# A hybrid attention layer: merge factors stored and loaded on another queue, exponents made in PSUM, two statistics steps moved

## The chip, the cores and the metric

The kernel runs on one core of one Trainium2 chip. The metric is device time in microseconds (us). The core has five engines with a queue of instructions each: PE (matmul), DVE (vector), ACT (scalar), POOL (GpSimd) and SP, which here only starts transfers (DMA). An engine works its instructions in order. A transfer is started by an instruction on the queue of SP or ACT and then runs by itself.

## The reference

One decoder layer for a prompt of 2048 positions and 32 sample rows, all in float32. For the part that matters here, each of 8 heads takes three dilated windows over the prompt, (128, 1), (512, 4) and (2048, 16), and the branch outputs are merged by their softmax denominators:

```
s = jnp.einsum('bnqrhc,bnkrhc->bnrhqk', qb, kc) * (HEAD_DIM ** -0.5) + bias
s = jnp.where(valid, s, NEG_INF)
lse = logsumexp(s, axis=-1)
o = einsum(exp(s - lse), vc)
...
w = jax.nn.softmax(jnp.stack(lses, axis=0), axis=0)
att = jnp.sum(w[..., None] * jnp.stack(outs, axis=0), axis=0)
...
x = x + jnp.concatenate([att, u * gate], axis=-1) @ w_out
x = x + _swiglu(x, norm2_g, w_gate, w_up, w_down)
```

Before it stands a projection of x to q, k, v, u and the gate; behind it the output projection and the feed-forward part.

## The kernel before

The stages follow each other: projections (to some 600 us of the span), attention over the prompt's heads (600 to 965), a junction in which the first block's output projection begins (to 1075), then output projection and feed-forward in three blocks of positions to the end. Each stage is written out by hand: `at(step, phase, fn)` puts a function into a plan, and the plan emits the instructions sorted by step and by phase, in the order early, exp, low, scores, turn, mid, values, out, misc, store. There is no reordering later; each engine's order is the order of emission.

In attention one step is one item. An item is a block of 128 queries of one head over its dense and 4-strided keys together ("band", at most 640 keys), or four residues of the 16-strided window ("strided"); there are 16 of the one and 4 of the other, 20 steps per head. For an item at step x, PE makes the scores (L864 band, L941 strided), DVE adds the bias and takes the maximum at x+1 (L870, L946 and L948), POOL subtracts it for strided items (L949), ACT takes the exponential (L875 at x+2, L952 at x+3), PE transposes the result (L891 at x+3, L961 at x+4), ACT and DVE copy it out of PSUM (L896, L963, L902), and PE multiplies with the values (L918, L970). DVE sums the strided item's exponentials (`strided_sum`, L956) at x+4. POOL gathers the strided keys and queries of an item, three casts (L933), two steps ahead of its scores.

When a head is done, `Stats` combines the statistics of its two parts in the next head's steps (s0 is that head's first step). `a` spreads the band part's maxima and sums over a masked tile sm (L995), `b` transposes them with two small matmuls (L1001), `c` copies the result to SBUF (L1005), `weights_a` forms the exponents (L1011 to L1013), `weights_e` takes their exponential on ACT (L1016), `weights_b` divides (L1021 to L1025), and `store` writes two factors per position to f_d in HBM (L1029, on ACT's queue). `merge_load` reads them back, each row repeated for 64 partitions, in four chunks of 512 positions with two loads of 128 KB each (L1042), on ACT's queue for heads 0 to 5 and half of head 6, on SP's behind that. `merge` multiplies and adds on POOL (L1051, L1053, L1055; ob is the band output, o the strided one), and `merge_store` writes the head to cat_d on SP (L1060). The chunks' tiles come from a ring of two ("pair") and at the end from two rings of three ("raw", "zn").

SP's queue in this stage holds the next head's loads of q, k (L824), bias rows (L829, tile b) and, in every second head, values (L815, 1 MB each), then merge_store, and in the last head eight loads of w_out (L1299, 256 KB each), which ACT and POOL split for the junction (L134 and L137, tile op). After that come load_cat (L1324), which reads cat_d back for the first output blocks, and the last factors.

The last head has its strided items early and its statistics in two halves: positions 0 to 63 of each residue at x+14 to x+16, the rest behind its end.

Of the kernel before, what the change touches and what calls it, by code (L numbers as in the profile page):

```python
# [64 lines left out]
def hymba_step(ctx: ExitStack, tc: tile.TileContext, A: dict, O: dict):  # L65
# [108 lines left out]
    def raw_tile():  # L174
        return rp.tile([P, 512], F32, name="raw", tag="raw", bufs=RAW)
# [809 lines left out]
    class Stats:  # L985
# [6 lines left out]
        def a(self):  # L992
            n = self.r1 // 8
            self.m = ap_.tile([P, 2 * P], F32, name="sm", tag="sm", bufs=1).rearrange("p (a n g) -> p a n g", a=2, g=8)[:, :, 0:n]
            dve.tensor_tensor(self.m, self.st["t"][:, 0:2, 0:n].unsqueeze(3).broadcast_to([P, 2, n, 8]),  # L995
                              sel_g.unsqueeze(1).unsqueeze(1).broadcast_to([P, 2, n, 8]), op=OP.mult)

        def b(self):
# [2 lines left out]
                pe.matmul(pt[0:self.r1, z * NT:(z + 1) * NT], self.m[:, z].rearrange("p n g -> p (n g)"), sel_r, start=True, stop=True)  # L1001

        def c(self):
            self.s = self.small("s12", 2)
            dve.tensor_copy(self.s.rearrange("p a t -> p (a t)"), self.p[0:self.r1, 0:2 * NT])  # L1005

        def weights_a(self):

            m3 = self.st["t"][0:self.r1, 2, :]
            self.f = f = self.small("f", 3)  # L1010
            dve.tensor_tensor(f[:, 2, :], self.s[:, 0, :], m3, op=OP.min)  # L1011
            dve.tensor_sub(f[:, 0, :], f[:, 2, :], self.s[:, 0, :])
            dve.tensor_sub(f[:, 1, :], f[:, 2, :], m3)  # L1013

        def weights_e(self):
            act.activation(self.f[:, 0:2, :], self.f[:, 0:2, :], AF.Exp)  # L1016
# [1 line left out]
        def weights_b(self):  # L1018
            f, m = self.f, self.f[:, 2, :]
            dd = self.small("dd", 2)  # L1020
            dve.tensor_mul(dd[:, 0, :], f[:, 0, :], self.s[:, 1, :])  # L1021
            dve.tensor_mul(dd[:, 1, :], f[:, 1, :], self.st["t"][0:self.r1, 3, :])
            dve.tensor_add(m, dd[:, 0, :], dd[:, 1, :])
            dve.reciprocal(m, m)
            dve.tensor_mul(f[:, 0:2, :], f[:, 0:2, :], m.unsqueeze(1).broadcast_to([self.r1, 2, NT]))  # L1025

        def store(self):
            n = self.r1 - self.r0
            act.dma_start(dap(f_d, self.h * 2 * T + self.r0 * NT, [[NT, n], [T, 2], [1, NT]]), self.f[self.r0:self.r1, 0:2, :])  # L1029


    mf = {}
# [1 line left out]
    def merge_load(h, ch):  # L1034

        if h < H - 2 or h == H - 2 and ch < 2:
            f = pair_tile(F32)
            mf[h, ch] = tuple(f[:, z, 0:256] for z in range(2))
        else:
            mf[h, ch] = tuple(t_[:, 0:256] for t_ in (raw_tile(), zn_tile()))  # L1040
        for z, t_ in enumerate(mf[h, ch]):
            (act if h < H - 2 or h == H - 2 and ch < 2 else sync).dma_start(  # L1042
                t_, dap(f_d, (h * 2 + z) * T + ch * 512, [[256, 2], [0, C], [1, 256]]))

    def merge(h, ch, eng, part=None):
        f1, f3 = mf[h, ch]
# [88 lines left out]
    def stats_of(h, steps, r0, r1):  # L1135
        d = {}
        at(*steps[0], lambda: d.update(s=Stats(h, sts[h], r0, r1)))
        for (y, ph), fn in zip(steps, "a b c weights_a weights_e weights_b store".split()):
            at(y, ph, lambda fn=fn: getattr(d["s"], fn)())

    for h in range(H):

        s0 = B0 + (h + 1) * NI
        end = h == H - 1
        ahead = h == H - 2
        if end:

            x = s0 - NI
            stats_of(h, [(x + y, ph) for y, ph in ((14, "early"), (14, "turn"), (15, "early"), (15, "misc"), (16, "early"), (16, "early"), (16, "mid"))], 0, 64)
            steps = ((2, "early"), (2, "turn"), (3, "early"), (4, "early"), (4, "early"), (5, "early"), (5, "early"))  # L1150
            at(x + 18, "mid", merge_load, h, 0)
            at(x + 18, "mid", merge_load, h, 1)
            for part in range(3):
                at(x + 20 + part, "store", merge, h, 0, dve, part)
                at(x + 21 + part, "store", merge, h, 1, pool, part)
            at(x + 24, "store", merge_store, h, 0, 2)
        else:
            steps = ((2, "misc"), (3, "misc"), (4, "early"), (4, "early"), (5, "early"), (5, "misc"), (6, "mid"))
# [614 lines left out]
    def first_block(B):  # L1773
# [1 line left out]
        m2, m1 = acc_place(2), acc_place(4)  # L1775
        load_cat(B, 1, 0, KD, m1)
        merge_load(h, 2)
        merge_load(h, 3)
        load_cat(B, 2, 0, KD, m2)
        B.place()  # L1780
        load_cat(B, 3, 0, KD)
# [261 lines left out]
```

## Time and profile before

| | us |
|---|---|
| runs | 2667.13, 2670.01, 2673.22 (median 2670.01) |
| profiled execution | 2675.66 |
| its span | 2673.9 |
| PE busy in the span | 2528.4 (95%) |
| DVE, ACT, POOL busy | 1341.9, 1179.1, 1348.5 |
| mean granted clock of PE | 0.966 |

In the rows, a number pair at the start is the start and the duration in us; x is the count; square brackets hold how long the engine was idle before and what it waited for; ACTq and SPq are instructions that start transfers. A row of waits has engine, tile and line, then what it waited for, the total us, how often, and the longest.

### The profile page before, as it was taken

To read this page: it belongs to the slowest core of one execution; us is meant where nothing else is said; L and a number is where in the kernel's file an instruction comes from. 1 tells how busy PE (TensorE), PEld (TensorE's weight loads), DVE (VectorE), ACT (ScalarE), POOL (GpSimd) and SP (SyncE) were. 2 spreads that over 40 slices of the span, in tenths; PEclk is the share of its full clock that TensorE was granted. 3 is DMA by queue.
4 is the path that set the end of the run, shared out by engine and by line. 5 is a ranking of instruction groups with operands and counts; after the bars stand their busy time and mean duration, and the time that the engine had idled before them with its cause. 6 is when DMAs were issued, how large, how long until landed. Compare 5 with 4: busy or idle time off the path is not lost.

```text
span 2673.9 us, 39478 instructions
## 1 busy us (share of the span) xinstructions
PE 2528.4 (95%) x14058; PEld 2194.8 (82%) x14058; DVE 1341.9 (50%) x2691; ACT 1179.1 (44%) x2513; POOL 1348.5 (50%) x1040
## 2 busy tenths in 40 slices
PE   8998899998989878999999999999999999999997
PEld 6777777677777657899999987999999988999996
DVE  3258784436666634444444364444444464344445
ACT  6414344435655536545454545332332334433333
POOL 1035553123656633776675743554454533666663
PEclk9999899999989988999999999999999997899999
DMA  8764844675435254455364554455463642555553
GB/s 246 215 208 154 250 140 140 180 247 183 140 125 174 62 156 127 142 166 189 129 208 140 178 175 136 162 168 186 147 208 125 222 145 90 181 203 195 203 196 117
DMA packets 292040, 451.73 MB, mean 169 GB/s; under 512 B 26087, under 2 KB 166552, under 8 KB 286724
## 3 DMA queue, kind: packets, MB, share of 16 engines
q1 hardware_dynamic: 277772, 433.34, 50.0%
q10 hardware_dynamic: 14072, 15.86, 2.0%
q8 instruction: 112, 1.84, 0.3%
q14 instruction: 84, 0.69, 0.1%
HBM read 361.79 MB, written 157.45 MB: 194 GB/s over the span
## 4 chain that ended last, share of the span: by engine, by line
PE 53%; POOL 8%; issue 7%; ACT 4%; DMA 4%; DVE 4%; SPq 1%; ACTq 1%; POOLq 0%; DVEq 0%
PE ps_o L1618 12%; PE ps_m L1545 8%; PE ps_m L1547 8%; PE ps_m L1546 8%; POOL op L1488 2%; DMA ab_d<-pair 2%; PE ps_o L918 2%; ACT fr L1456 1%; PE ps_s L864 1%; PE ps_s L941 1%; PE ps_t L891 1%; ACTq L1042 1%; POOL pair L1468 1%; POOL fr L1471 1%; POOL dw L137 1%
## 5 line engine op out<-in xcount | busy, mean ns | idle before, releaser
L1488 POOL TENSOR_TENSOR op<-fr,op 128x512 fp32r<-128x512 f32 x385 | 489.0, 1301 | 338.9 <-ACT op L1484 308.4
L1545 PE MATMUL ps_m<-xh,op 128*128 128x384 f32 (+4 forms) x1932 | 626.1, 324 | 0.0
L1546 PE MATMUL ps_m<-xl,op 128*128 128x384 f32 (+4 forms) x1932 | 624.3, 323 | 0.0
L1547 PE MATMUL ps_m<-xh,op 128*128 128x384 f32 (+4 forms) x1932 | 624.2, 323 | 0.0
L1618 PE MATMUL ps_o<-dw,hw 128*128 128x512 f32 x2040 | 485.9, 393 | 12.7 <-DVE acc L1620 11.7
L1618 PEld LDWEIGHTS ps_o<-dw,hw 128*128 128x128 f32 x2040 | 380.5, 188 | 95.6 <-DVE acc L1620 18.0
L1546 PEld LDWEIGHTS ps_m<-xl,op 128*128 128x128 f32 x1932 | 375.0, 194 | 4.0
L1545 PEld LDWEIGHTS ps_m<-xh,op 128*128 128x128 f32 x1932 | 374.6, 194 | 4.2
L1547 PEld LDWEIGHTS ps_m<-xh,op 128*128 128x128 f32 x1932 | 374.2, 194 | 0.2 <-POOL op L1488 0.2
L1620 DVE TENSOR_TENSOR acc<-acc,ps_o 128x512 f32<-128x512 f32 (+1 forms) x362 | 247.0, 686 | 216.8 <-PE ps_o L1618 216.8
L1585 ACT ACTIVATE ps_t<-zn 128x384 f32<-128x384 f32 (+1 forms) x126 | 58.3, 462 | 473.7 <-DVE zn L1568 368.3
L1484 ACT ACTIVATE op<-fr 128x512 fp32r<-128x512 f32 x396 | 235.9, 623 | 25.1 <-DMA fr<-ab_d 18.4
L137 POOL TENSOR_TENSOR dw<-fd,dw 128x1024 fp32r<-128x1024 f32 x66 | 158.9, 2407 | 124.6 <-ACT dw L134 124.5
L317 PE MATMUL ps_s<-wh,xh 128*128 128x512 f32 x480 | 197.4, 411 | 6.4 <-ACT xh L134 5.9
L318 PE MATMUL ps_s<-wl,xh 128*128 128x512 f32 x480 | 191.9, 400 | 1.3 <-DVE wl L225 1.3
L319 PE MATMUL ps_s<-wh,xl 128*128 128x512 f32 x480 | 191.4, 399 | 0.0
L1488 POOL TENSOR_TENSOR op<-pair,op 128x512 fp32r<-128x512 f32 x63 | 81.6, 1304 | 116.9 <-ACT op L1484 116.9
L1595 ACT ACTIVATE hw<-ps_t 128x384 fp32r<-128x384 f32 (+1 forms) x126 | 56.1, 453 | 176.6 <-DVE ps_t L1591 175.6
L317 PEld LDWEIGHTS ps_s<-wh,xh 128*128 128x128 f32 x480 | 92.7, 193 | 36.2 <-issue 8.3
L318 PEld LDWEIGHTS ps_s<-wl,xh 128*128 128x128 f32 x480 | 92.9, 193 | 20.1 <-DVE wl L225 2.8
L319 PEld LDWEIGHTS ps_s<-wh,xl 128*128 128x128 f32 x480 | 92.3, 192 | 20.4 <-DVE xl L137 0.2
L603 POOL TENSOR_TENSOR vl<-kv,vh 100x512 fp32r<-100x512 f32 (+1 forms) x32 | 45.5, 1424 | 123.5 <-PE ps_t L613 40.9
(440 smaller groups left out, 4495.0 us busy)
## 6 DMA issues: line engine op xcount, KB each, us to landing
fr<-ab_d SPq DMA_DIRECT2D x308, 256.0 KB
fd<-in_w_down_dram SPq DMA_DIRECT2D x66, 512.0 KB
out_ks_dram<-in_cache_k_dram SPq DMA_DIRECT2D x56, 512.0 KB
out_vs_dram<-in_cache_v_dram SPq DMA_DIRECT2D x56, 512.0 KB
ab_d<-fr SPq DMA_DIRECT2D x88, 256.0 KB
raw<-in_w_in_dram SPq DMA_DIRECT2D x72, 256.0 KB
qk_d<-pair SPq DMA_DIRECT2D x64, 256.0 KB
ab_d<-pair SPq DMA_DIRECT2D x63, 256.0 KB
```

The lines of the kernel that those rows point to most:

```text
L137: (eng_lo or pool).tensor_sub(lo, src, hi.bitcast(F32))
L317: pe.matmul(o[j], xh[:, k, :], wh, start=(k == 0), stop=False)
L318: pe.matmul(o[j], xh[:, k, :], wl, start=False, stop=False)
L319: pe.matmul(o[j], xl[:, k, :], wh, start=False, stop=(k == KD - 1))
L1484: act.activation(ops[f, j][0], ab[f][j], AF.Copy)
L1488: (pool if f or j in POOL_LOW else dve).tensor_sub(lo_, ab[f][j], hi.bitcast(F32))
L1545: pe.matmul(out, wh[:, ks], xh[:, :, k], start=(k == 0), stop=False)
L1546: pe.matmul(out, wh[:, ks], xl[:, :, k], start=False, stop=False)
L1547: pe.matmul(out, wl[:, ks], xh[:, :, k], start=False, stop=(k == 3))
L1585: act.activation(g, c, AF.Silu)
L1618: pe.matmul(ps[0:nr], l_, r_[:, cs], start=(z == 0 and y == 0), stop=(z == FC - 1 and y == len(pairs) - 1))
L1620: dve.tensor_add(B.acc[i][0:nr, cs], B.acc[i][0:nr, cs], ps[0:nr])
```

## The change

Six edits. `Stats.a` runs on POOL instead of DVE. `c` and `weights_a` become one step: the difference of the two maxima is written into PSUM, both exponents are made from there, and one sum is copied to SBUF. The factors' store is issued by SP. `merge_load` loads two chunks at once (four loads) into the two halves of a tile, and all on SP; it is called at s0+8 and s0+11 instead of s0+8, 8, 14 and 17 (20 for head 6). `strided_sum` moves from phase "low" to phase "mid" of its step, which is behind the bias of that step's other item.

```
-            dve.tensor_tensor(self.m, self.st["t"][:, 0:2, 0:n]...
+            pool.tensor_tensor(self.m, self.st["t"][:, 0:2, 0:n]...
...
         def c(self):
-            self.s = self.small("s12", 2)
-            dve.tensor_copy(self.s.rearrange("p a t -> p (a t)"), self.p[0:self.r1, 0:2 * NT])
-        def weights_a(self):
-            m3 = self.st["t"][0:self.r1, 2, :]
+            p, m3, x = self.p[0:self.r1], self.st["t"][0:self.r1, 2, :], self.p[0:self.r1, 2 * NT:3 * NT]
+            self.s = self.small("s1", 1)[:, 0, :]
             self.f = f = self.small("f", 3)
-            dve.tensor_tensor(f[:, 2, :], self.s[:, 0, :], m3, op=OP.min)
-            dve.tensor_sub(f[:, 0, :], f[:, 2, :], self.s[:, 0, :])
-            dve.tensor_sub(f[:, 1, :], f[:, 2, :], m3)
+            dve.tensor_tensor(x, p[:, 0:NT], m3, op=OP.subtract)
+            dve.tensor_scalar(f[:, 0, :], x, -1.0, 0.0, op0=OP.mult, op1=OP.min)
+            dve.tensor_scalar(f[:, 1, :], x, 0.0, None, op0=OP.min)
+            dve.tensor_copy(self.s, p[:, NT:2 * NT])
...
         def store(self):
-            act.dma_start(dap(f_d, ...), self.f[self.r0:self.r1, 0:2, :])
+            sync.dma_start(dap(f_d, ...), self.f[self.r0:self.r1, 0:2, :])
...
     def merge_load(h, ch):
         if h < H - 2 or h == H - 2 and ch < 2:
             f = pair_tile(F32)
-            mf[h, ch] = tuple(f[:, z, 0:256] for z in range(2))
+            t_ = f[:, 0], f[:, 1]
         else:
-            mf[h, ch] = tuple(t_[:, 0:256] for t_ in (raw_tile(), zn_tile()))
-        for z, t_ in enumerate(mf[h, ch]):
-            (act if h < H - 2 or h == H - 2 and ch < 2 else sync).dma_start(
-                t_, dap(f_d, (h * 2 + z) * T + ch * 512, [[256, 2], [0, C], [1, 256]]))
+            t_ = raw_tile(), zn_tile()
+        for c in range(2):
+            mf[h, ch + c] = tuple(x[:, c * 256:(c + 1) * 256] for x in t_)
+            for z, x in enumerate(mf[h, ch + c]):
+                sync.dma_start(x, dap(f_d, (h * 2 + z) * T + (ch + c) * 512, [[256, 2], [0, C], [1, 256]]))
...
-            for ch, (a, b) in enumerate(((8, 11), (8, 14), (14, 17), (20, 24) if ahead else (17, 20))):
-                at(s0 + a, "mid", merge_load, h, ch)
+            for ch, (a, b) in enumerate(((8, 11), (8, 14), (11, 17), (11, 24) if ahead else (11, 20))):
+                if ch % 2 == 0:
+                    at(s0 + a, "mid", merge_load, h, ch)
...
-            at(x + 4, "low", strided_sum, it)
+            at(x + 4, "mid", strided_sum, it)
```

What moves on SP's queue, first in a head with value loads (the fourth head's steps; v and ve are value tiles, qh, k and ql the next head's queries and keys, f the factors). Before:

```order
L824 DMA qh<-qk_d 128x1x2048
L824 DMA k<-qk_d 128x1x2048
L824 DMA ql<-qk_d 128x1x2048
L1060 DMA cat_d<-ob 256x1x256 x2
L829 DMA b<-b_d 128x768
L815 DMA v<-v_d 128x16x128
L815 DMA ve<-v_d 128x16x128
```

After:

```order
L824 DMA qh<-qk_d 128x1x2048
L824 DMA k<-qk_d 128x1x2048
L824 DMA ql<-qk_d 128x1x2048
L1059 DMA cat_d<-ob 256x1x256 x2
L829 DMA b<-b_d 128x768
L1027 DMA f_d<-f 128x2x16
L1042 DMA pair<-f_d 128x1x256 x4
L815 DMA v<-v_d 128x16x128
L1042 DMA pair<-f_d 128x1x256 x4
L815 DMA ve<-v_d 128x16x128
```

The factors' store and all eight loads have come between the bias rows and the value loads.

On SP in the last head, before (here v is the tile that w_out's parts are staged in):

```order
L1060 DMA cat_d<-ob 256x1x256 x2
L1299 DMA v<-in_w_out_dram 128x512 x8
L1042 DMA raw<-f_d 128x1x256
L1042 DMA zn<-f_d 128x1x256
L1324 DMA pair<-cat_d 128x7x128
L1060 DMA cat_d<-ob 64x2x256 x2
```

And after:

```order
L1059 DMA cat_d<-ob 256x1x256 x2
L1027 DMA f_d<-f 128x2x16
L1298 DMA v<-in_w_out_dram 128x512 x4
L1042 DMA pair<-f_d 128x1x256 x4
L1042 DMA raw<-f_d 128x1x256
L1042 DMA zn<-f_d 128x1x256
L1042 DMA raw<-f_d 128x1x256
L1042 DMA zn<-f_d 128x1x256
L1298 DMA v<-in_w_out_dram 128x512 x4
L1027 DMA f_d<-f 64x2x16
L1323 DMA pair<-cat_d 128x7x128
L1059 DMA cat_d<-ob 64x2x256 x2
```

Four of the eight w_out loads now stand behind head 6's eight factor loads, and both factor stores of the end are on this queue.

On POOL at the end of a merge, where the next head's third step stands, before:

```order
L1051 TENSOR_TENSOR ob<-ob,pair 128x256
L1053 TENSOR_TENSOR o_7090<-o_7090,pair 128x16x16
L1055 TENSOR_TENSOR ob<-ob,o_7090 128x256
L949 TENSOR_TENSOR e_7877<-e_7877,st 128x512
L933 COPY sq<-k 128x512
```

After:

```order
L1050 TENSOR_TENSOR ob<-ob,pair 128x256
L1052 TENSOR_TENSOR o_7090<-o_7090,pair 128x16x16
L995 TENSOR_TENSOR sm<-st,sel_g 128x256
L1054 TENSOR_TENSOR ob<-ob,o_7090 128x256
L949 TENSOR_TENSOR e_7869<-e_7869,st 128x512
```

The masked statistics stand behind the merge's second part, so they also wait for that part's factors.

More of the change, by code (lines that the diff above doesn't have):

```diff
@@ L994, in a @@
             self.m = ap_.tile([P, 2 * P], F32, name="sm", tag="sm", bufs=1).rearrange("p (a n g) -> p a n g", a=2, g=8)[:, :, 0:n]
-            dve.tensor_tensor(self.m, self.st["t"][:, 0:2, 0:n].unsqueeze(3).broadcast_to([P, 2, n, 8]),
+            pool.tensor_tensor(self.m, self.st["t"][:, 0:2, 0:n].unsqueeze(3).broadcast_to([P, 2, n, 8]),
                               sel_g.unsqueeze(1).unsqueeze(1).broadcast_to([P, 2, n, 8]), op=OP.mult)
@@ L1020, in weights_b @@
             dd = self.small("dd", 2)
-            dve.tensor_mul(dd[:, 0, :], f[:, 0, :], self.s[:, 1, :])
+            dve.tensor_mul(dd[:, 0, :], f[:, 0, :], self.s)
             dve.tensor_mul(dd[:, 1, :], f[:, 1, :], self.st["t"][0:self.r1, 3, :])
@@ L1028, in store @@
             n = self.r1 - self.r0
-            act.dma_start(dap(f_d, self.h * 2 * T + self.r0 * NT, [[NT, n], [T, 2], [1, NT]]), self.f[self.r0:self.r1, 0:2, :])
+            sync.dma_start(dap(f_d, self.h * 2 * T + self.r0 * NT, [[NT, n], [T, 2], [1, NT]]), self.f[self.r0:self.r1, 0:2, :])
     mf = {}
@@ L1137, in stats_of @@
         at(*steps[0], lambda: d.update(s=Stats(h, sts[h], r0, r1)))
-        for (y, ph), fn in zip(steps, "a b c weights_a weights_e weights_b store".split()):
+        for (y, ph), fn in zip(steps, "a b c weights_e weights_b store".split()):
             at(y, ph, lambda fn=fn: getattr(d["s"], fn)())
@@ L1148, in hymba_step @@
             x = s0 - NI
-            stats_of(h, [(x + y, ph) for y, ph in ((14, "early"), (14, "turn"), (15, "early"), (15, "misc"), (16, "early"), (16, "early"), (16, "mid"))], 0, 64)
-            steps = ((2, "early"), (2, "turn"), (3, "early"), (4, "early"), (4, "early"), (5, "early"), (5, "early"))
+            stats_of(h, [(x + y, ph) for y, ph in ((14, "early"), (14, "turn"), (15, "early"), (16, "early"), (16, "early"), (16, "mid"))], 0, 64)
+            steps = ((2, "early"), (2, "turn"), (3, "early"), (4, "early"), (5, "early"), (5, "early"))
             at(x + 18, "mid", merge_load, h, 0)
-            at(x + 18, "mid", merge_load, h, 1)
             for part in range(3):
@@ L1157, in hymba_step @@
         else:
[L1158 to L1161 removed]
+            steps = ((2, "misc"), (3, "misc"), (4, "early"), (5, "early"), (5, "misc"), (6, "mid"))
+            for ch, (a, b) in enumerate(((8, 11), (8, 14), (11, 17), (11, 24) if ahead else (11, 20))):
+                if ch % 2 == 0:
+                    at(s0 + a, "mid", merge_load, h, ch)
                 for part in range(3):
```

1 line of the change is left out of this document (removed).

## The prediction

> **What bounds the kernel now.** I read the page first, then the waits of PE in the attention stage (640 to 950 us of the span), then single stalls in the timelines, then the transfers. The page:
>
> ```profile
> span 2673.9 us, 39478 instructions
> PE 2528.4 (95%) x14058; PEld 2194.8 (82%) x14058; DVE 1341.9 (50%) x2691; ACT 1179.1 (44%) x2513; POOL 1348.5 (50%) x1040
> ```
>
> PE bounds the whole, so only idle PE time can be won. All that is edited lies in the attention stage and its junction with the first output block. Who lets PE idle there (total us, times, longest):
>
> ```profile
> PE ps_s L864 <- DVE st L870: 7.9, 6, 1.9
> PE ps_t L961 <- ACT e L952: 6.7, 8, 1.6
> PE ps_o L961 <- ACT e L952: 5.7, 3, 3.7
> PE ps_s L941 <- DVE st L870: 3.2, 2, 2.5
> PE ps_o L918 <- ACT o L979: 2.9, 1, 2.9
> ```
>
> Two causes, once per head each. The first is ACT, blocked while it issues the four factor loads; here the head with the worst case, with PE's clock beside it (columns of the stretches: length, busy time of PE, PEld, DVE, ACT, POOL, granted clock, DMA share, GB/s):
>
> ```profile
> 742.52 5.46 ACTq L1042 DMA_DIRECT2D pair<-f_d  x4
> 749.36 0.66 PE L961 MATMUL ps_o<-ident,e 128*128 128x128 f32 x4 [3.73 <-ACT e L952]
> 771.82 0.66 PE L961 MATMUL ps_o<-ident,e 128*128 128x128 f32 x4 [0.35 <-ACT e L952]
> 687.60:694.00 6.40, 6.24 (x62) 4.65 (x57) 4.82 (x11) 2.80 (x10) 5.15 (x7) 1.00 0.99 403
> 713.20:719.60 6.40, 6.40 (x63) 5.30 (x62) 3.91 (x11) 4.60 (x11) 6.32 (x8) 1.00 0.12 40
> 745.20:751.60 6.40, 2.52 (x17) 1.70 (x16) 1.49 (x4) 3.57 (x9) 1.93 (x3) 0.87 0.13 45
> 751.60:758.00 6.40, 6.40 (x46) 5.90 (x48) 3.49 (x8) 3.16 (x8) 0.88 (x2) 0.60 0.11 36
> 828.40:834.80 6.40, 6.19 (x28) 5.35 (x29) 3.55 (x10) 2.71 (x6) 1.55 (x2) 0.50 1.13 287
> 706.71 0.66 PE L961 MATMUL ps_t<-ident,e 128*128 128x128 f32 x4 [1.46 <-ACT e L952]
> 706.80:713.20 6.40, 6.25 (x61) 5.15 (x62) 5.10 (x11) 5.09 (x13) 1.68 (x2) 1.00 0.14 45
> ```
>
> ACT sits 5.46 us in four issues, PE waits 3.73 us, and then the clock is at 0.87 and 0.60 for two stretches: 6.4 x (0.13 + 0.40) = 3.4 us more. Behind a wait of 1.46 us the clock stayed at 1.00 (last two rows). Of all such stretches from 640 to 900, four drops stand out, each in a head of its own, the last at 828.4. The 0.35 us kind of wait, five of the eleven on ACT e L952, is not of this cause. The second cause is DVE, which makes the exponents ahead of the next bias:
>
> ```profile
> 688.31 1.11 POOL L1053 TENSOR_TENSOR o<-o,pair 128x256 f32<-128x256 f32 x1
> 691.87 0.19 DVE L1005 COPY s<-ps_t 128x32 f32<-128x32 f32 x1 [0.51 <-PE ps_t L1001]
> 692.10 0.51 DVE L1011 TENSOR_TENSOR f<-s,st 128x16 f32<-128x16 f32 x1
> 692.64 0.97 DVE L1012 TENSOR_TENSOR f<-f,s 128x16 f32<-128x16 f32 x1
> 693.53 1.05 DVE L1013 TENSOR_TENSOR f<-f,st 128x16 f32<-128x16 f32 x1
> 695.11 0.55 PE L864 MATMUL ps_s<-k,qh 128*128 128x384 f32 x2 [1.27 <-DVE st L870]
> 695.59 0.16 DVE L1021 TENSOR_TENSOR dd<-f,s 128x16 f32<-128x16 f32 x1
> 694.49 1.07 POOL L933 CAST sq<-ql 128x512 fp32r<-128x512 f32 x1
> ```
>
> Sixteen columns cost 0.97 and 1.05 us while POOL's cast runs (it ends at 695.56) and 0.16 us right after: two SBUF operands stall against POOL, the copy from PSUM (0.19) does not.
>
> How long a head takes, by the statistics' matmul of the second window and of the last one, five heads apart:
>
> ```profile
> 691.21 0.62 PE L1001 MATMUL ps_t<-sel_r,sm 128*128 128x16 f32 x4
> 907.67 0.62 PE L1001 MATMUL ps_o<-sel_r,sm 128*128 128x16 f32 x4
> ```
>
> 216.5 / 5 = 43.3 us per head. The stalls of the two causes are 7.9 + 3.2 + 6.7 + 5.7 - 5 x 0.35 = 21.7 us over six heads, 3.6 each; the four drops of the clock, 3.4 us or a little less, are another 2.2 per head. Without them a head is 43.3 - 5.8 = 37.5 us.
>
> **The change part by part.**
>
> *Issues taken off ACT, exponents in PSUM.* ACT loses 52 loads and 9 stores, DVE's step becomes four instructions of about 0.19 us instead of 0.19 + 0.51 + 0.97 + 1.05 = 2.72. If the second stall (1.27 us) goes, 1.5 us of saving covers it; bounds of the four: 0.8 us (L1005's price) and 2.7 us (no gain). I take 0.8, since each reads PSUM as L1005 does. Together the cap is 6 x 5.8 = 35 us.
>
> *Masked statistics on POOL.* The nearest row is POOL's 128x256 merge, 1.11 us, nine times. It comes just behind that merge (done at 689.42) and PE wants it at 691.21: hidden by 0.7 us, unless that merge is late. Bounds for the nine: 0 and 9 x 1.1 = 10 us; I take 0 here and count lateness below. *Strided sum behind the bias:* same instruction; what DVE waited for it now covers with the bias, but the waits of PE above show DVE only at the exponents, once per head. Gain and cost 0, bounds -1.8 (the five waits of 0.35) and +1.8 (as many more).
>
> *Loads moved onto SP's queue.* This is what takes most back. How these loads run one behind the other shows at the junction, where they are on SP already:
>
> ```profile
> 948.23 0.53 SPq L1042 DMA_DIRECT2D raw<-f_d  x1
> 953.10 0.42 DVE L1051 TENSOR_TENSOR ob<-ob,raw 128x256 f32<-128x256 f32 x1 [0.48 <-DMA raw<-f_d]
> 956.58 0.61 DVE L1053 TENSOR_TENSOR o<-o,zn 128x256 f32<-128x256 f32 x1 [2.72 <-DMA zn<-f_d]
> 962.51 0.90 POOL L1053 TENSOR_TENSOR o<-o,zn 128x256 f32<-128x256 f32 x1 [2.21 <-DMA zn<-f_d]
> 975.40 2.80 SPq L1324 DMA_DIRECT2D accm<-cat_d  x1
> 984.63 0.87 POOL L1053 TENSOR_TENSOR o<-o,zn 128x256 f32<-128x256 f32 x1 [2.37 <-DMA zn<-f_d]
> 986.16 1.06 ACT L1329 ACTIVATE accm<-accm 128x1024 fp32r<-128x1024 f32 x1 [12.36 <-DMA accm<-cat_d]
> ```
>
> First landing 4.8 us after its issue, then one per 3.0 us ((962.5 - 956.5) / 2). In the stretch from 713.2 such loads alone keep a DMA share of 0.12: two of 16 engines. And the 512 KB load issued at 975.40 behind four of them lands at 986.1, after the last of these (984.6): whatever follows them on SP's queue waits on those two engines.
>
> [...]
>
> What the two engines carry per head after the change: 8 x 3.0 = 24 us of factor loads; q, k (3 MB), cat_d, bias rows and half of two value loads, together about 5.1 MB, at 403 GB/s 12.7 us, with 512-byte rows slower, say 13.5; and they run dry between the factors' store and the first load: a first landing takes 4.8 - 3.0 = 1.8 us beyond its transfer, and store and load each pay it, so about 4 us (bounds 2.5 to 5). Sum 41.5 us per head, against 37.5 for PE. Late factors reach PE because POOL works in order:
>
> ```profile
> 886.12 1.04 POOL L949 TENSOR_TENSOR e<-e,st 128x512 f32<-128x512 f32 x1 [2.59 <-DVE st L948]
> 892.25 1.11 PE L941 MATMUL ps_s<-sq 128*128 128x128 f32 x8
> ```
>
> POOL has 2.6 us to spare ahead of L949; behind it come two merge parts and the three casts of the next gather, 1.04 + 2 x 0.9 + 3 x 1.07 = 6.05 us, and PE's matmul on them starts 6.1 us after L949: no slack. So merges more than about 2.6 us late stall PE. Six heads: 6 x 41.5 - 10 us that the first head has in hand (its engines begin empty) = 239, plus 5 for one or two clock drops = 244, against 6 x 43.3 = 260: **-16 us**.
>
> *The last head.* Its factor store and eight factor loads now stand among the eight loads of w_out, four before and four behind:
>
> ```profile
> 909.47 27.17 SPq L1299 DMA_DIRECT2D v<-in_w_out_dram  x8
> 915.85 0.36 ACTq L1029 DMA_DIRECT2D f_d<-f  x1
> 937.86 0.62 ACT L134 ACTIVATE op<-v 128x512 fp32r<-128x512 f32 x1
> 945.93 0.88 POOL L1055 TENSOR_TENSOR ob<-ob,o 128x256 f32<-128x256 f32 x1
> ```
>
> Store at 915 (1 us earlier, in the time base of before), factors from 920, the eighth landing at 920 + 8 x 3.05 + 0.9 = 945, the fifth w_out load at about 946, where ACT wants it at 937.86. From there to the merge that releases SP's next store (946.8) it was 9 us; I take 7.5, since ACT no longer waits there to issue the first half's factor store: 953.5 instead of 946.8, less 1 us of POOL's work that is earlier, **+6 us** (bounds -5, if these loads overtake, to +8). PE starts that head about 1 us later through POOL: **+1**. Behind it the chain (merge, store to cat_d, load, 986.16) is as long as before: (7,0) and (7,1) still load one by one, and the statistics on POOL, 3 us later there, end before that chain.
>
> Sum: -16 + 6 + 1 = -9 us. The profiled execution took 2675.66 us, 5.65 above the median 2670.01 of the runs; from the median I say 2661.
>
> **The rivals.**
> (1) The queue costs nothing. For it: POOL has slack, SP idles, and issue time on SP is free. Then the cap is won: -35, and the last head another -2 (ACT's 2.9 us stall less POOL's extra work): 2633. [...] Against it: the load at 975.40.
> (2) Slower: the clock. Where POOL's lateness idles PE by 1.3 to 2.5 us at a place, the clock may drop in each head instead of in four of six: 37.5 + 4 + 3.4 = 44.9 us x 6 = 269, +9, with the last head's +7 2686; since slower heads also let the transfers catch up, I price it at half of the nine, 2681. It decides from about five drops on. For it: four heads of six had one. Against it: none behind the 1.46 us.
> [...]
> (3) No change: gains of 16 eaten by a last head of +12 to +15 (POOL and ACT both behind the late w_out loads): 2668.
>
> **How the numbers follow.** Forecast 0.48 (2650 to 2670), rival 1 0.2, rival 2 0.18, rival 3 0.14. A change of 0.2% (5.3 us) is about what a measurement of this kernel can tell from none. The forecast's own range lies three quarters beyond it: faster 0.36 + 0.2 = 0.56, same 0.12 + 0.12 = 0.24, slower 0.20. Range 2635 to 2680: it reaches to the two outer cases and leaves out half of each, 0.19.
>
> **What would show it.** Right: no ACT wait above 1 us at L961; DVE's four small instructions under 1 us together; POOL waiting for pair<-f_d in every second head at least; heads alternating between 38 (with value loads) and 42; ACT waiting several us for v<-in_w_out_dram. Wrong: heads all at 37.5 with POOL not waiting (rival 1), or a clock under 0.9 in most heads (rival 2).

## The result, and the profile after

The changed kernel takes 2659.4 us (median of 11 runs, 2641.8 to 2667.7) against 2670.0 (11 runs, 2665.7 to 2676.7) beside it: a ratio of 0.995, 95% interval 0.9927 to 0.9974. The forecast was 2661. The number fits. Of its reasons, the loss in the last head is right, the gain in the heads is smaller than forecast, and some 5 us come from a stage in which nothing is edited.

The two profiled executions lie further apart than the medians, 2646.70 us against 2675.66. One row of each says why: a stretch in the feed-forward stage, where nothing is edited (columns of the stretches: length, busy time of PE, PEld, DVE, ACT, POOL, granted clock, DMA share, GB/s; before first, then after).

```profile
2216.00:2296.00 80.00, 75.63 (x359) 69.18 (x358) 31.12 (x102) 35.91 (x83) 25.90 (x20) 0.70 0.24 78
```

```profile
2216.00:2296.00 80.00, 75.26 (x486) 68.93 (x485) 40.17 (x115) 38.00 (x90) 39.93 (x30) 0.91 0.38 129
```

A drop of the clock at the border of two token blocks cost 80 x 0.30 = 24 us in the one and 80 x 0.09 = 7 us in the other. It is long in ten of the fourteen traces of this case and short in four (after, e2, e8, e9). These 17 us are left out of what follows, but that they have nothing to do with the edits is not shown: all four are kernels with the new exponents, and of the eleven executions of after three (2641.8 to 2646.7) stand 10 us below the other eight, while before's eleven form one group. The median of the other eight is 2663.1, 6.9 us below before. Each kernel has one trace, and before's traced execution is 5.65 us above its median, so the parts of a gain are known to a few us only.

The waits of PE in the attention stage after the change (640 to 950 us; total us, times, longest):

```profile
PE ps_s L941 <- POOL sq L933: 11.1, 15, 1.3
PE ps_o L918 <- ACT o L979: 9.0, 1, 9.0
PE ps_t L961 <- ACT e L952: 3.5, 7, 0.9
PE ps_s L941 <- DVE e L946: 2.8, 1, 2.8
```

Both old causes are gone: nothing waits at L864 for DVE, and the longest wait at L961 is 0.9 us instead of 3.7. In their place PE waits for POOL's gather (L933), and once for 9.0 us. POOL is late because it waits for the factors (640 to 900 us), and ACT waits for w_out in the last head:

```profile
POOL ob L1050 <- DMA pair<-f_d: 22.2, 12, 4.8
POOL o L1052 <- DMA pair<-f_d: 20.2, 15, 2.9
```

```profile
933.38 0.63 ACT L134 ACTIVATE op<-v 128x512 fp32r<-128x512 f32 x1 [11.23 <-DMA v<-in_w_out_dram]
934.34 2.40 PE L918 MATMUL ps_o<-pt,v 128*64 128x256 f32 x12 [9.01 <-ACT o L979]
980.73 0.80 PE L1337 MATMUL ps_m<-op,accm 128*128 128x512 f32 x1 [7.03 <-ACT accm L1328]
```

The heads by the statistics' matmul, the first window and the last, six heads apart, with before's first window as the third row:

```profile
645.92 0.62 PE L1001 MATMUL ps_o<-sel_r,sm 128*128 128x16 f32 x4
894.43 0.62 PE L1001 MATMUL ps_o<-sel_r,sm 128*128 128x16 f32 x4
647.06 0.62 PE L1001 MATMUL ps_o<-sel_r,sm 128*128 128x16 f32 x4
```

248.5 us for six heads, 41.4 each (before, from 647.06 to 907.67: 260.6, 43.4 each). The clock still drops in them, once in each of the five heads behind the first and each time right behind two waits for POOL's gather; here the two waits in one of these heads and the stretch behind them:

```profile
794.18 0.33 PE L941 MATMUL ps_s<-sq 128*128 128x128 f32 x1 [0.89 <-POOL sq L933]
795.16 1.50 PE L941 MATMUL ps_s<-sq 128*128 128x128 f32 x7 [0.66 <-POOL sq L933]
793.60:800.00 6.40, 5.16 (x28) 4.71 (x30) 2.46 (x7) 2.79 (x7) 4.24 (x6) 0.73 0.14 45
```

6.4 x 0.27 = 1.7 us each, 8.5 us in five heads, against 3.4 us in each of four heads before.

Then the last head gives most of it back: to the matmul on accm that waits, 980.73 - 894.43 = 86.3 us against 79.6 before (987.27 - 907.67; before's row):

```profile
987.27 0.79 PE L1338 MATMUL ps_m<-op,accm 128*128 128x512 f32 x1 [5.20 <-ACT accm L1329]
```

At the next wait of PE that both kernels have, in the first block behind the junction, the lead is 6.7 us (first before, then after):

```profile
1062.18 1.12 PE L1405 MATMUL ps_t<-ident,pair 128*128 128x128 f32 x4 [4.65 <-ACT pair L1391]
```

```profile
1055.52 1.75 PE L1404 MATMUL ps_t<-ident,pair 128*128 128x128 f32 x7 [4.67 <-ACT pair L1390]
```

That is all that the edited stage brings in these two traces. The other gain stands in the products of the feed-forward stage; here the costliest group of the stretch 1700 to 2150, in which PE is busy throughout at a clock of 1.00, in before and in after (busy us, mean ns of one):

```profile
L1546 PE MATMUL ps_m<-xl,op 128*128 128x384 f32 x549 | 185.7, 338 | 0.0
```

```profile
L1546 PE MATMUL ps_m<-xh,op 128*128 128x384 f32 x549 | 183.8, 335 | 0.0
```

The same matmul is 3 ns shorter, on three lines with 549 each: 1647 x 3 ns = 5 us in these 450 us. What of it reaches the time shows by DVE's additions to acc: the last one of the first block, and the 256th of 385 that read ps_o, late in the second block (first before, then after).

```profile
1582.10 0.69 DVE L1636 TENSOR_TENSOR acc<-acc,ps_m 128x512 f32<-128x512 f32 x1
2144.34 0.69 DVE L1620 TENSOR_TENSOR acc<-acc,ps_o 128x512 f32<-128x512 f32 x1 [0.68 <-PE ps_o L1618]
```

```profile
1575.66 0.69 DVE L1635 TENSOR_TENSOR acc<-acc,ps_m 128x512 f32<-128x512 f32 x1
2131.11 0.69 DVE L1619 TENSOR_TENSOR acc<-acc,ps_o 128x512 f32<-128x512 f32 x1 [0.68 <-PE ps_o L1617]
```

The lead is 6.4 us at the end of the first block, no more than at 1062, and 13.2 us late in the second. Of the 6.8 between, 1.7 are a shorter drop of the clock at the border of the two blocks (granted clock from 1640 to 1720: 0.94 and 0.96), and 5.1 are left for the products. In the first block the same matmul is 3 ns shorter too, and no lead comes of it. No line of this stage is in the diff.

### The profile page after: what moved, and what is told of

Same layout as the page of the kernel before. It is cut to its first block, busy times and chain, and to the rows that moved or that the text cites. A ratio compares the mean times of both kernels' runs of the same rounds, so it can differ in the third digit from the quotient of the medians.

```text
span 2644.6 us, 39468 instructions
## 1 busy us (share of the span) xinstructions
PE 2493.3 (94%) x14058; PEld 2162.8 (82%) x14058; DVE 1332.9 (50%) x2682; ACT 1177.2 (45%) x2513; POOL 1351.1 (51%) x1049
## 4 chain that ended last, share of the span: by engine, by line
PE 49%; POOL 8%; issue 8%; DMA 7%; DVE 4%; ACT 3%; SPq 3%; POOLq 0%; ACTq 0%; DVEq 0%
PE ps_o L1617 12%; PE ps_m L1546 7%; PE ps_m L1544 7%; PE ps_m L1545 7%; POOL op L1487 2%; DMA ab_d<-pair 2%; DMA pair<-f_d 2%; SPq L1042 2%; ACT fr L1455 1%; DMA f_d<-f 1%; PE ps_o L918 1%; POOL pair L1476 1%; POOL pair L1467 1%; POOL fr L1470 1%; POOL dw L137 1%
## 5 line engine op out<-in xcount | busy, mean ns | idle before, releaser
L1544 PE MATMUL ps_m<-xh,op 128*128 128x384 f32 (+4 forms) x1932 | 613.3, 317 | 0.0
L1546 PE MATMUL ps_m<-xh,op 128*128 128x384 f32 (+4 forms) x1932 | 612.4, 317 | 0.0
L1545 PE MATMUL ps_m<-xl,op 128*128 128x384 f32 (+4 forms) x1932 | 612.0, 317 | 0.0
L1617 PE MATMUL ps_o<-dw,hw 128*128 128x512 f32 x2040 | 486.5, 393 | 16.4 <-DVE acc L1619 15.1
L1544 PEld LDWEIGHTS ps_m<-xh,op 128*128 128x128 f32 x1932 | 366.8, 190 | 4.1
L1545 PEld LDWEIGHTS ps_m<-xl,op 128*128 128x128 f32 x1932 | 366.6, 190 | 3.6
L1546 PEld LDWEIGHTS ps_m<-xh,op 128*128 128x128 f32 x1932 | 366.3, 190 | 0.1
```

The costliest lines, as they stand in the source:

```text
L1544: pe.matmul(out, wh[:, ks], xh[:, :, k], start=(k == 0), stop=False)
L1545: pe.matmul(out, wh[:, ks], xl[:, :, k], start=False, stop=False)
L1546: pe.matmul(out, wl[:, ks], xh[:, :, k], start=False, stop=(k == 3))
L1617: pe.matmul(ps[0:nr], l_, r_[:, cs], start=(z == 0 and y == 0), stop=(z == FC - 1 and y == len(pairs) - 1))
```

## The experiments

Each was timed in five rounds beside the kernel before; the ratio stands with its 95% interval. "Heads" is the mean of heads between statistics matmuls (L1001) in the profiled execution.

| kernel | median us | ratio to before | heads us |
|---|---|---|---|
| before | 2670 to 2677 | 1 | 43.4 |
| after | 2659.4 | 0.995 (0.9927 to 0.9974) | 41.4 |
| e3 queue alone | 2669.5 | 0.9987 (0.9972 to 1.0002) | 41.8 |
| e12 exponents alone | 2656.2 | 0.9929 (0.9902 to 0.9956) | 42.7 |
| e2 all but the queue | 2654.0 | 0.9924 (0.9896 to 0.9953) | 42.9 |
| e5 spread loads alone, on ACT | 2669.4 | 0.9977 (0.9965 to 0.9990) | 46.0 |
| e1 after, loads spread | 2607.1 | 0.975 (0.9728 to 0.9772) | 37.9 |
| e6 queue and spread loads | 2629.2 | 0.9823 (0.9801 to 0.9845) | 38.9 |
| e10 after, spread, 8 issues on ACT | 2623.5 | 0.9791 (0.9766 to 0.9817) | 40.1 |
| e4 after, w_out ahead | 2652.3 | 0.9915 (0.9897 to 0.9934) | 41.6 |
| e7 e1, masked statistics on DVE | 2608.1 | 0.9744 (0.9713 to 0.9775) | 38.0 |
| e8 e1, strided sum ahead of the bias | 2617.3 | 0.9782 (0.9760 to 0.9805) | 38.5 |
| e9 e1, 8 issues on SP | 2610.4 | 0.9755 (0.9742 to 0.9769) | 37.9 |
| e11 e1, factors side by side | 2614.5 | 0.9764 (0.9751 to 0.9777) | 38.0 |

**The parts apart: e3, e2, e12.** The queue's move alone:

```diff
-            act.dma_start(dap(f_d, ...), self.f[self.r0:self.r1, 0:2, :])
+            sync.dma_start(dap(f_d, ...), self.f[self.r0:self.r1, 0:2, :])
...
-            (act if h < H - 2 or h == H - 2 and ch < 2 else sync).dma_start(
+                sync.dma_start(x, dap(f_d, ...))     # two chunks per step, as in the change
```

> The kernel before with only the move of the factors' store and loads to SP's queue, with the tiles and steps of the changed kernel; exponents on SBUF, masked statistics on DVE and the strided sum in its old phase. Theory: ACT's stalls at L961 go and the two engines' transfers set the heads at 41 to 42 us on average, so DVE's stalls of about 1.8 us a head are partly hidden in them; the last head is 6 us longer: 2670 - 5 = 2665, 0.998. Rival 1 (the stalls add up, none is hidden): 2670 minus the gain of the changed kernel that the exponents don't bring, 2660 or less. Rival 2 (the queue takes all back): 2670 to 2676.

Measured 2669.5, 0.9987, 3.8 us below before where the theory had 5. The interval holds both the theory's 0.998 and rival 2's 1.000, so the time alone doesn't decide between them. The trace has the theory's mechanism: PE's waits at L961 are nearly gone (3.9 us), the heads are 1.6 us shorter each, 250.9 instead of 260.6 over six, and the last head takes it back, with PE waiting 11.3 us at L918 for ACT, which waits 12.0 us for w_out. The theory had DVE's stall partly hidden; it is not, PE waits 8.2 us at L864.

The other way round, all but the queue (e2: the lines above as before, all else as in the change):

> The changed kernel with the factors' store and loads given back to ACT's queue, at the steps and in the tiles of before; exponents, masked statistics and strided sum stay as changed. Theory (two separate causes of stalls in PE): ACT's blocked issues are back with PE's waits at L961 (12.4 us before, 4.6 in the changed kernel) and clock drops in about four heads, while the stalls on DVE's exponents (11.1 us before) stay away; the last head is as before: 2670 - 8 = 2662, 0.997. Rival 1 (the queue alone brought the gain): 2670, 1.000. Rival 2 (the queue brought nothing, and the exponents all of it): 2655 or less, since the last head's 6.7 us are saved too.

Measured 2654.0, 0.9924. This kernel is no slower than the changed one; rival 2, the exponents all of it, has the time. But its six executions form two groups, 2643.4 to 2648.5 and 2659.5 to 2663.5, as the short and the long drop of the clock would make them (the traced one, 2643.4, has the short one), and the theory's 2662 lies in the upper group. Its heads are only 0.5 us shorter than before. PE's waits (640 to 950):

```profile
PE ps_t L961 <- ACT e L952: 13.5, 8, 5.3
PE ps_o L961 <- ACT e L952: 7.3, 3, 5.1
PE ps_s L941 <- DVE st L870: 3.3, 6, 0.8
```

L864 has 1.0 us left of 7.9, and L961, which had 12.4 us before, has 20.8: what DVE no longer holds up, ACT's four issues do. So the exponents alone:

```diff
-            dve.tensor_copy(self.s..., self.p[0:self.r1, 0:2 * NT])
...
-            dve.tensor_tensor(f[:, 2, :], self.s[:, 0, :], m3, op=OP.min)
-            dve.tensor_sub(f[:, 0, :], f[:, 2, :], self.s[:, 0, :])
-            dve.tensor_sub(f[:, 1, :], f[:, 2, :], m3)
+            dve.tensor_tensor(x, p[:, 0:NT], m3, op=OP.subtract)
+            dve.tensor_scalar(f[:, 0, :], x, -1.0, 0.0, op0=OP.mult, op1=OP.min)
+            dve.tensor_scalar(f[:, 1, :], x, 0.0, None, op0=OP.min)
+            dve.tensor_copy(self.s, p[:, NT:2 * NT])
```

> The kernel before with only the exponents made in PSUM (four small instructions of DVE in place of four slower ones, one step earlier); factors on ACT's queue, masked statistics on DVE, strided sum in its old phase. Theory (stalls in one head don't add: what DVE no longer takes, ACT's four issues take): the waits at L864 on st L870 fall from 7.9 us to under 1.5, those at L961 rise from 12.4 to about 18, heads stay at 43 and the time within 6 us of before, 0.998. Rival (the two causes add up, as the forecast had it): L961 stays at 12.4, heads at 42, and with a drop or two of the clock less 2660 or below, 0.995 or less.

Measured 2656.2, 0.9929. The time is the rival's, the trace is not (PE, 640 to 950):

```profile
PE ps_t L961 <- ACT e L952: 9.9, 8, 2.8
PE ps_s L941 <- DVE st L870: 7.8, 6, 1.8
PE ps_o L961 <- ACT e L952: 6.5, 3, 4.1
PE ps_s L864 <- DVE st L870: 1.0, 1, 1.0
```

The waits moved, from L864 to L941 and L961, as the theory said of L961 (12.4 to 16.4), and the six heads are 4.4 us shorter (256.2). The rest of its 17 us is not there. By the additions to acc its lead over before is 7.9 us at the end of the first block (1574.20) and 17.3 at the 256th (2127.00). About 5 of these 9.4 us are the clock, which drops at the border of the two blocks in before (0.94 from 1640 to 1720) and not in e12 (1.00); some 4 are left for the products. The same group as above, 1700 to 2150, in e12, and in e3 below it:

```profile
L1545 PE MATMUL ps_m<-xh,op 128*128 128x384 f32 x549 | 183.8, 335 | 0.0
```

```profile
L1548 PE MATMUL ps_m<-xh,op 128*128 128x384 f32 x546 | 184.6, 338 | 0.0
```

335 ns with the new exponents, 338 with the old ones, in all fourteen traces: 335 in after, e1, e2, e4 and e7 to e12; 338 in before, e3, e5 and e6.

**The two engines: e5, e1, e6.** Each factor load is cut into two, so that the outermost dimension of the access is 64 rows and no longer 2:

```diff
-                sync.dma_start(x, dap(f_d, ..., [[256, 2], [0, C], [1, 256]]))
+                for y in range(2):
+                    sync.dma_start(x[y * C:(y + 1) * C], dap(f_d, ... + y * 256, [[0, C], [1, 256]]))
```

> The changed kernel with every factor load cut into two, one per 64 partitions (16 loads of 64 rows per head in place of 8 of 2 x 64); all else as in the changed kernel. Theory (the loads are slow because only two engines carry each, 3.0 us apiece, and they hold up what stands behind them on SP's queue): cut this way all engines share a load, POOL's waits for pair<-f_d fall from 42 us to under 15, the six heads from 248 to about 235, and the last head loses its 6.7 us because the w_out loads 5 to 8 come on time: 13 + 6 below the changed kernel, about 2641, 0.989 of before. Rival (the loads' own time doesn't matter, what is late is their place behind the q and k loads and the wait for the store): POOL still waits over 30 us for pair<-f_d and the time stays within 3 us of the changed kernel, 2656 to 2662.

Measured 2607.1, 0.975: 52 us below the changed kernel, where the theory hoped for 18. POOL's waits for pair<-f_d are gone altogether, the clock is at 1.00 from 640 to 900, and the heads stand at the floor (the second and the third row are four heads apart):

```profile
640.00:900.00 260.00, 249.41 (x2238) 200.68 (x2234) 180.92 (x450) 175.08 (x448) 180.90 (x196) 1.00 0.47 153
687.59 0.62 PE L1001 MATMUL ps_t<-sel_r,sm 128*128 128x16 f32 x4
837.90 0.62 PE L1001 MATMUL ps_t<-sel_r,sm 128*128 128x16 f32 x4
1007.92 1.97 PE L1405 MATMUL ps_t<-ident,pair 128*128 128x128 f32 x8 [4.67 <-ACT pair L1391]
```

(837.90 - 687.59) / 4 = 37.6 us per head; the sixth takes 40.1. The wait at L1405 comes 47.6 us earlier than in after. The six heads bring 21.1 of that, the last head and the junction behind it 31.2, and e1 enters the stage 4.7 us later. In the junction the merge loads stand in the chain that PE waits for, and they were slow too: between the last window and the wait at L1405 POOL waits 22.9 us for raw and zn in after, 7.6 us in e1. Up to 18 of the 31 us are the clock, which was 0.87 on the mean of that stretch in after (161.1 us) and 0.98 in e1 (129.9 us). The loads alone keep a DMA share of 0.13 and 42 GB/s in after (701 to 713 us), which is 2.1 of 16 engines, and 0.25 and 85 GB/s in e1 (694.5 to 700.5 us), 4.0 engines; in e9 below, where the loads are cut the same way and joined two by two, the share reaches 0.59, 9.4 engines, and 169 GB/s (692 to 695 us). So the loads with 2 outermost keep two engines busy and the cut ones more; that the outermost dimension sets their number, and that 64 of it reach all engines, was the author's estimate (the loads of q and k, with 128, keep a share of 0.98, before, 687 to 690 us). That all 16 take part in a cut load no row shows.

The cut alone, with the loads left on ACT:

> The kernel before with only the cut of each factor load into two of 64 rows; the loads stay on ACT's queue at their old steps, and exponents, masked statistics and strided sum are as before. Theory (ACT's stall is the time of issuing, the two engines hurt SP's transfers and the junction): eight issues of 0.6 to 0.7 us stand where four took 5.46 us, so the waits at L961 stay near 12 us and the heads at 42 to 43; only the last head and the junction win, about 20 us: 2650, 0.991. Rival (ACT was held by the slow transfers in front of its queue, not by issuing): the waits at L961 fall under 4 us and the heads to about 40: 2630, 0.984.

Measured 2669.4, 0.9977: a far smaller gain than either had. The waits at L961 rise to 23.1 us, since twice as many issues hold ACT longer (below, the issues of before for 8 loads of one head, then of e5 for 16).

```profile
742.52 5.46 ACTq L1042 DMA_DIRECT2D pair<-f_d  x4
759.80 1.06 ACTq L1042 DMA_DIRECT2D pair<-f_d  x2
765.78 1.04 ACTq L1042 DMA_DIRECT2D pair<-f_d  x2
```

```profile
749.28 4.99 ACTq L1043 DMA_DIRECT2D pair<-f_d  x8
766.70 2.39 ACTq L1043 DMA_DIRECT2D pair<-f_d  x4
773.87 2.40 ACTq L1043 DMA_DIRECT2D pair<-f_d  x4
```

With the cut an issue takes 0.6 us, but sixteen are 9.8 us of ACT per head against 7.6 before, and the heads grow to 46.0. The last head and the junction win nearly what the theory said, 18 us up to the first matmul on woh (86.9 us from the last window instead of 105.2), and the six heads take 15 back (275.7 instead of 260.6). So neither the queue alone (-4 us) nor the cut alone (-6) is worth much; together, with the old exponents:

> The kernel before with the factors' store and loads on SP's queue and the loads cut into two of 64 rows; exponents on SBUF, masked statistics on DVE and the strided sum in its old phase. It differs from the kernel of 2607 us (e1) by the statistics alone. Theory (with the transfers out of the way DVE's stall on the exponents sets the head): PE waits about 8 to 11 us for st L870 before 900, heads of 39 to 40 us against 37.6, with some clock drops: 2607 + 14 = 2621, 0.981. Rival (the exponents are worth nothing): 2607 or less, 0.975. Rival 2 (each such stall drops the clock): 2635.

Measured 2629.2, 0.9823, 46 us below before. Between the theory's 2621 and rival 2's 2635; PE waits 7.3 us at L864 for st L870, and a head takes (837.56 - 683.34) / 4 = 38.6 us, 1.0 more than e1's, 6 us in six heads. The clock is at 1.00 in these heads too, so the four drops of before went with ACT's stall. How much of the 1.0 is the exponents is not shown apart: the strided sum is in its old phase too, and e8 below puts that at 0.6. Of the 22 us between the medians the two traces show 12.7 (spans 2617.7 and 2604.9): 4.2 up to the first addition to acc, 5.5 at the end of the first block and 12.2 at the 256th, most of the last step by the products (338 and 335 ns). The rest lies between the execution of e6 that was traced, its fastest (2619.5), and its median.

**What issuing costs ACT: e9, e10, e11.** One load brings both chunks of a factor for 64 partitions, 8 issues per head (e9 on SP, e10 on ACT):

```diff
+            for y in range(2):
+                QUEUE.dma_start(x[y * C:(y + 1) * C].rearrange("p (c w) -> p c w", w=256),
+                                dap(f_d, ... + y * 256, [[0, C], [512, 2], [1, 256]]))
```

> The changed kernel with the loads of e1 joined two by two: one load per factor and 64 partitions brings both chunks of a merge (64 rows of 2 x 1 KB), so there are 8 issues per head, as in the kernel before, and all engines carry each. Theory (issues on SP cost nothing, since SP idles): as e1, 2601 to 2613, heads of 37.6. Rival (SP's time of issuing, some 6 us for eight, delays what follows): heads the same, last head and junction shorter, 2600 or less.

> The kernel of e9 with the factors' store and the loads of heads 0 to 6 back on ACT's queue: eight issues per head on ACT as before, but on all engines. Theory (each issue holds ACT, 0.65 to 0.7 us when nothing is in front of it, 1.4 us when the two engines' queue is full): four in a row hold it 2.7 us in place of 5.46, the waits at L961 fall from 20.8 us (e2) to about 8, heads of 40: 2607 + 15 = 2622, 0.981. Rival 1 (ACT was held by the slow transfers alone): heads of 37.6, 2607. Rival 2 (ACT is held by any four loads as long): heads of 43, 2645.

e9 measured 2610.4, 0.9755 (0.9742 to 0.9769), as e1: half as many issues on SP change nothing. e10 measured 2623.5, 0.9791, with heads of 40.1, as its theory had it:

```profile
694.62 2.58 ACTq L1039 DMA_DIRECT2D pair<-f_d  x4
700.12 0.58 ACTq L1039 DMA_DIRECT2D pair<-f_d  x1
700.73 2.42 ACTq L1039 DMA_DIRECT2D pair<-f_d  x3
```

On ACT, 5.6 us of issues per head lengthen it by 2.2 us over e1's 37.9. L961 has less than the 8 us that was expected (5.1), since part of the waits went to L891 (PE ps_t L891 <- ACT e L875, 5.6 us in all).

e11 keeps the two factors side by side in DRAM, so that two loads of 2 KB rows bring a pair of merges:

> The changed kernel with the factors kept in DRAM as 256 of one and 256 of the other in turn, so that a merge's four rows come in two loads of 64 x 2 x 2 KB on all engines (two stores per head instead of one, four loads instead of eight; in the junction four loads of 64 x 2 KB per merge pair). Theory (in the heads PE is the bound at 37.6 us; only the junction, where POOL waits 7 us for raw<-f_d, can still win from a shorter transfer): 2604, within 0.3% of e1. Rival (the second store and both factors coming together make the first merge later): 2610 to 2615.

Measured 2614.5, 0.9764 (0.9751 to 0.9777): within 0.3% of e1, as the theory said, but in the rival's 2610 to 2615; the intervals of the two kernels overlap, so the time does not decide. Nothing more is won: four heads take 37.6 us each, as in e1, and POOL still waits 7.5 us for raw<-f_d.

**The last head: e4.**

```diff
-                    at(s0 + a, "mid", merge_load, h, ch)
+                    at(*((s0 + 14, "store") if ahead and ch else (s0 + a, "mid")), merge_load, h, ch)
```

> The changed kernel with one step moved: in the last head the second four factor loads of the head before are issued three steps later, behind the w_out loads 5 to 8. Theory (those four loads hold up w_out by 4 x 3.0 us): ACT's wait of 11.2 us and POOL's of 13.4 us for v<-in_w_out_dram fall below 3 us, PE's 9.0 us wait at L918 goes, and about 6 us of the 6.7 that the last head lost are had back: 2653, 0.9937. Rival (w_out is late because its staging buffers come free late, or the chain through the last merges sets the end): no gain, 2658 to 2661, the wait merely stands elsewhere.

Measured 2652.3, 0.9915, as the theory's 2653. PE's wait at L918 is gone, ACT's for w_out too, POOL's is 2.9 us. A new one of 7.9 us stands at the second statistics matmul, behind POOL's merge (the row), yet from the last window (893.68) to it the last head takes 52.6 us instead of 61.5.

```profile
946.30 1.03 PE L1001 MATMUL ps_t<-sel_r,sm 128*128 128x16 f32 x4 [7.93 <-POOL sm L995]
```

**The small moves: e7, e8**, each undone in e1 (`pool.tensor_tensor` back to `dve.tensor_tensor` for sm; "mid" back to "low" for strided_sum).

> The kernel of e1 with the masked statistics back on DVE, nothing else. Theory (POOL does them for nothing in the heads and costs PE 2 us once behind the last head, where L1001 waits for sm L995): heads 37.6 still, the end 2 us earlier, DVE's eight of 0.6 us hidden: 2605, within 0.2% of e1. Rival (they cost DVE its slack ahead of the bias): 0.6 us more wait at st L870 per head, and now and then a clock drop: 2612 or more.

> The kernel of e1 with the strided sum back in its old phase, ahead of the step's bias. Theory (no stall in the trace before hung on it): within 0.2% of e1, 2602 to 2612, with PE's waits for st L870 and e L946 within 2 us of e1's 3.9 us. Rival (it delays the bias by its 0.68 us, and now that nothing else holds a head up PE waits for it): 28 times 0.3 to 0.7 us, 2615 to 2625.

e7: 2608.1, 0.9744 (0.9713 to 0.9775), the same as e1. e8: 2617.3, 0.9782 (0.9760 to 0.9805), 10 us above e1's median and on the rival's side, but its interval overlaps e1's. The trace shows the rival's mechanism: PE's waits for st L870 and e L946 are 9.3 us instead of 3.9 (640 to 900), and four heads take 839.34 - 686.61 = 152.7 us instead of 150.3, 0.6 us a head. The six heads account for some 4 of the 10. Part of the rest is the clock behind the heads (from 1000 to 1100 us 0.93 against e1's 0.97, from 1590 to 1690 0.97 against 1.00), and that this has to do with the strided sum is not shown.

```profile
PE ps_s L941 <- DVE st L870: 6.5, 6, 1.1
PE ps_s L941 <- DVE e L946: 2.8, 1, 2.8
```

## Why the prediction was right, and where it was not

**The floor of a head.** 37.5 us, worked out from the stalls and the clock drops, stands in e1 as 37.6, four heads in a row. Right, for a kernel in which POOL does not wait for factors; in the changed kernel only the first head (38.2) came near it.

**Two causes, cap 35.** As a sum for the cap it held: e1's six heads are 33.2 us shorter than before's. The two are not alike, though. With the exponents alone (e12) the six heads win 4.4 us, since PE's waits turn up at L961 for ACT (12.4 to 16.4 us) and at L941 for DVE (3.2 to 7.8); e2, with the strided sum moved too, has 20.8 us at L961. With ACT's stall gone and the old exponents (e6) they win 27.3 us, the clock drops with it, and DVE's wait at L864 stays as large as before (7.3 us).

**The two engines on SP's queue.** 41.5 us per head was forecast with 5 us in all for clock drops beside it, and the heads after the first (645.92 to 684.12, 38.2 us) average 42.1 with 8.5 us of drops in them. The term that was mis-sized is the "10 us that the first head has in hand": it had 3, and the next head, 43.1, nothing. So the heads brought 12 us, not 16. Nor do they alternate cleanly between 38 and 42: 38.2, 43.1, 40.3, 42.1, 41.4, 43.4. e1 shows the cause: the same bytes, in the same queue at the same steps, make POOL wait 0 us for pair<-f_d instead of 42.4 once each load is cut. The allowance for the value loads' 512-byte rows has its row too: they ran at 297 GB/s (before, 739 to 742 us), where q and k ran at 401 (687 to 690 us).

**Rival 2's drops.** What the rival needed, a drop in each head behind waits for POOL, came in five heads of six. But each was half as long as before's (1.7 us lost, not 3.4), so they cost 8.5 us and not the 20 that the rival counted, and no head's mean clock is below 0.95. The forecast had 5 us for one or two long drops; five short ones came near that by luck, since no step had them shorter, and why they were is not shown.

**The last head.** +6 in the last head and +1 ahead of it forecast, 6.7 measured by the same two rows, with ACT and POOL waiting 11 and 13 us for w_out; e4, which moves one step behind those loads, has a last head 9 us shorter. Right.

**Masked statistics at no cost:** right in the heads and in the time (e7); in the last head PE waits once, 2.2 us, for POOL's sm. **Strided sum, gain and cost 0:** wrong where PE bounds the head, worth 0.6 us a head in e8, since the bias behind it came late; in the changed kernel, whose heads wait for POOL, it was not tried by itself.

**DVE's four instructions.** Forecast 0.8 us; the rows of after (640 to 900) give 0.182 + 0.174 + 0.162 + 0.163 = 0.68. The last two rows are the second product behind the exponents, in after and in before:

```profile
L1008 DVE TENSOR_TENSOR ps_t<-ps_t,st 128x16 f32<-128x16 f32 x4 | 0.7, 182 | 2.9 <-PE ps_t L1001 2.9
L1009 DVE TENSOR_SCALAR f<-ps_t 128x16 f32<-128x16 f32 x4 | 0.7, 174 | 0.1
L1011 DVE COPY s<-ps_t 128x16 f32<-128x16 f32 x4 | 0.7, 163 | 0.0
L1010 DVE TENSOR_SCALAR f<-ps_t 128x16 f32<-128x16 f32 x4 | 0.6, 162 | 0.0
L1020 DVE TENSOR_TENSOR dd<-f,st 128x16 f32<-128x16 f32 x6 | 5.6, 934 | 0.0
L1022 DVE TENSOR_TENSOR dd<-f,st 128x16 f32<-128x16 f32 x6 | 1.9, 319 | 0.0
```

They are the price of it that was not seen: the products behind the exponents now run beside POOL's casts (L933) in most heads, and this one takes 0.93 us on the mean where it took 0.32. No wait of PE stands behind them, but the factors' store does, so the loads start later by as much; what that costs was not measured.

**What the sum did not have.** The edited stage gave 6.7 us of the 9 forecast in the two traces. That the median came out 10.6 lower, near the 9, owes something to some 5 us in the feed-forward products, and to three executions 10 us below the others, neither of which any step looked for: the number was right in part by luck. The queue's move is worth 4 us by itself (e3, interval from -7.5 to +0.5) and nothing that the runs show on top of the other edits (0.995 against e2's 0.9924, whose intervals overlap).

**What stays open.** Why the feed-forward products take 335 ns. Nothing in their own code differs. By the code, the exponents' tile shrinks from 2 x 128 to 2 x 64 bytes per partition, which moves whatever is allocated behind it, the weight tiles op among them, by 128 bytes; every kernel with the small tile has 335 and every one with the large tile 338. That the placement is the cause was not tried: it needs a kernel that moves the tiles and nothing else. Open too are what makes the drop of the clock in the feed-forward stage long or short, whether the edits have a part in it, and e8's remainder over e1 (10 us, 4 accounted for).

## What to carry to other kernels

Before moving transfers to another queue, look at how many engines each one uses: here a load whose outermost dimension is 2 kept a DMA share of 0.13 (two of 16 engines, after), took 3.0 us (before, at the junction) and held up what stood behind it. Moving such loads was worth 4 us, cutting them in two 6, and the cut on top of the move 52. A wait that goes in one place can come back in another: e12 took DVE's stall at L864 away, and PE waited longer at L961 and L941, so it is worth asking which of two stalls sets the loop. The floor of the loop is worth working out first, since it tells when to stop. The fastest kernel here (e1, 2607 us, 0.975 of before) is the changed one with that cut.

## What the runs showed of the hardware

Four issues in a row on ACT's queue hold ACT 2.58 us with the cut loads (e10) and up to 5.46 us with loads that keep a DMA share of 0.11 to 0.14 (before). A matmul of 384 columns that nobody edited changed from 338 to 335 ns, in step with the size of a tile elsewhere. Two waits of 0.9 and 0.7 us close together had a drop of the clock behind them (0.73 from 793.6 to 800 us, after), where one of 1.46 us had none (1.00 from 706.8 to 713.2 us, before). And the border between the second and the third block costs 7 or 24 us in clock; among kernels with the cut, too, both lengths occur (e1 has the long one, its row below; e9 has the short one, with a mean clock of 0.983 over its span against e1's 0.978):

```profile
2160.00:2240.00 80.00, 75.25 (x404) 71.29 (x403) 30.63 (x100) 37.57 (x87) 36.33 (x29) 0.72 0.31 103
```
